# Weights laid out in DRAM by loads, and the first projections taken k tile by k tile

## The chip, the cores and the metric

The kernel runs on one core of a Trainium2 chip. The metric is the time of one execution on the device in microseconds (us). A core has a TensorE for matrix products (PE in the profile; its weight loads are PEld), a VectorE (DVE), a ScalarE (ACT), a GpSimd (POOL), a SyncE (SP) that only issues transfers here, and 16 DMA engines between DRAM and SBUF. Products are summed in eight PSUM banks. Each engine takes its instructions in program order and waits on semaphores of the others.

## The reference

One layer over 256 tokens `x` of width 1024, with 256 context tokens `ctx`. Everything is float32.

```
sh1, sc1, g1, sh2, sc2, g2 = split(silu(c) @ w_mod + b_mod)         # the context: the same with c_ctx
hc = rmsnorm(ctx) * (1 + csc1) + csh1
hx = rmsnorm(x) * (1 + sc1) + sh1
u, q, k, v, g, gates, lr = split(h @ w_in)                          # widths 512 512 512 1024 1024 2048 32
pooled = centred means of u over windows 2, 4, 8, 16, minus u
o = gated linear attention, both directions, of q, k, v, seeded by the context's k and v
x = x + g1 * mixer(pooled, o, g, gates) @ w_o                       # w_pool_br and w_gla_br inside
x = x + g2 * moe(rmsnorm(x) * (1 + sc2) + sh2)                      # 32 experts, 2 of one group per token
return rmsnorm(x) * final_g
```

The weights are 201 MB for the experts (`moe_w1`, `moe_w3`, `moe_w2`), 25 MB for `w_mod` and some 34 MB for the rest. They pass through SBUF once.

## The kernel before

**Stages.** (1) the modulation of the first norm and the projections u, q and half of g of the tokens; (2) k, v, the other half of g, the decays, attention, pooling, gates and the output projection, some 240 us in which the tokens (`hx`) and the context (`hc`) are matmul operands; (3) routing; (4) the experts in 16 pairs, whose hidden products are `hp` (line 1349) and whose outputs are `yp` (line 1382); (5) the last norm.

**Loads.** A load is one transfer of at most 1 MiB into a slot of 128 x 2048 floats (`ld`). The text `LOADS` lists the loads of stages 1 and 2 in order, and the experts' follow. The SP issues them in order; there are 20 slots in lane r (some hold other tiles) and 2 in lane m (for `mod` loads). A load is issued once its slot's last user is done, and eight transfers at most are under way, since each takes one of eight semaphores. `plan_loads` finds the step from which a load may be issued. `f` loads are 256 columns of `w_mod` for all eight k tiles, so each row brings 1 KB runs; `qu` loads are the columns of u and q for two k tiles (4 KB runs); `in` and `g` loads are 512 columns for four k tiles (2 KB runs); `mod` and experts' loads have 8 KB runs.

**Order of work.** The text `WORK` is the program of stages 1 to 3. Each item calls a step function (`steps`), and while it runs, the class `Line` chains each instruction on PE, ACT and DVE behind the last of its engine; so the items' order is the engine's order. A product is made of three passes in a rounded format: `s kind j` casts 1024 weights a partition on ACT (high part), `l kind j` subtracts on DVE (low part), then the products high x high, high x low, low x high run. There are three buffers for such parts (`highs`, `lows`, `third`, two halves each).

**Stage 1.** `s x` squares and sums x (ACT, DVE), `n x` sums over partitions with a matmul against ones (`ss_ps`) and makes the reciprocal root (ACT Ln, Exp; DVE `newton`). `f h j` (`first_cols`) multiplies one load of `w_mod` by the two condition columns, 8 matmuls into a bank `mod`, and copies the 256 columns to `sa`; `t j` (`shifted`) turns them into columns (`mcol`, `amul`) and calls `modulated`: DVE scales x, ACT adds the shift (`hx`, high part), DVE makes the low part; two k tiles at a time. `q j` and `u k` are the products. `i n` puts n idle matmuls of ones on PE (`g<-ones`). For the context there are `s c` (squares), `a c` (three sums), `n c` and `h i`. `e q` and `e u` copy the finished banks out on ACT and give the banks back; `k k 0` and `k k 1` are k's products for tokens and context, and their four banks are those of q and u.

Of the kernel before, what the change touches and what calls it, by code (L numbers as in the profile page):

```python
# [129 lines left out]
def hybrid_block_kernel(  # L130
    ctx: ExitStack,
    tc: tile.TileContext,
    x, xT, cT, vec, w_mod, b_mod, w_in, w_gates, pool_w,
    w_pool_br, w_gla_br, w_o, router_w, router_b,
# [333 lines left out]
    def first_cols(half, j):  # L468

        if half:  # L470
            first_ps[j] = bank("mod0")
        w, ps, hs = need(("first", half, j)), first_ps[j], slice(256 * half, 256 * half + 256)
        sm = sa[:, 512 * (j % 2):512 * (j % 2) + 512]
        with tc.high_priority():
            for k in range(KT):
                g = 32 * (k % 4)
                pe.matmul(ps[g:g + 32, hs], scol[:, k, :], w[:, 256 * k:256 * k + 256],
                               start=(k < 4), stop=(k > 3), tile_position=(0, g))
            if half + j:
                dve.tensor_copy(out=sm[:, hs], in_=ps[:, hs])  # L480
            else:
                act.copy(out=sm[:, hs], in_=ps[:, hs])
        done(("first", half, j))

    def shifted(j):

        ps = first_ps.pop(j)
        k2 = slice(2 * j, 2 * j + 2)
        with tc.high_priority():
            for h in range(2):  # L490
                for i in range(2):
                    n = 256 * h + 128 * i
                    pe.matmul(ps[:, 4 * h + 2 * i:4 * h + 2 * i + 2], sa[:, 512 * (j % 2) + n:512 * (j % 2) + n + 128], sums4,
                                   start=True, stop=True)
            dve.tensor_tensor(out=mcol[:, :, :, k2], in0=ps[:, 0:8].rearrange("p (h i u) -> p h u i", h=2, i=2),
                              in1=bmod[:, :, None, k2].to_broadcast([128, 2, 2, 2]), op=ALU.add)
            dve.scalar_tensor_tensor(out=amul[:, :, k2], in0=mcol[:, 1, :, k2], scalar=1.0,
                                     in1=g1n[:, None, k2].to_broadcast([128, 2, 2]), op0=ALU.add, op1=ALU.mult)
            modulated(xn, banks["rx"], 2 * j, 2, 0, hx)
        if j == 3:  # L500
# [1143 lines left out]
```

## Time and profile before

| | us |
|---|---|
| median of 3 runs (747.81 to 748.62) | 747.84 |
| the profiled execution | 749.17 |
| its span, first to last instruction | 747.5 |
| PE busy | 691.5 (93%) |
| DVE busy | 298.0 (40%) |
| ACT busy | 205.7 (28%) |
| DMA queue of the loads, share of 16 engines | 89.9% |

A busy PE is not PE at its peak, because matmuls are pipelined and their ends are modelled. One float32 matmul stands in the trace as two records; the rounded ones as one. A DMA share a little above 1 means that packets overlap. In the chain that ended last, PE has 69% of the span and transfers of experts' weights 24%; the rest is in single per cents. The page's DMA row, 40 slices of 18.7 us, reads 9, 9, 9, 7, 5, 4, 2, 3, 7 tenths at the start and 9 or 8 from the tenth slice (168 us) to the last but one.

### The profile page before, as it was taken

What the parts mean: (1) busy time and instruction counts of PE and PEld (TensorE: products, weight loads), DVE (VectorE), ACT (ScalarE), POOL (GpSimd) and SP (SyncE); (2) the same over time, 40 slices, a digit from 0 to 9 for tenths busy, and PEclk for the clock granted to TensorE, in tenths of its full rate; (3) what the DMA queues carried; (4) which work ended last, traced back from release to release, by engine and by line L of the source; (5) the groups of instructions that cost most, each with busy time, mean ns of one, the idle gap of its engine ahead of it and who ended that gap; (6) DMA issues with size and microseconds to landing.
All of it is one profiled execution on the core that took longest, in us unless ns stands there. A gap on an engine that the chain in (4) does not pass through costs nothing.

```text
span 747.5 us, 9833 instructions
## 1 busy us (share of the span) xinstructions
PE 691.5 (93%) x3986; PEld 393.9 (53%) x3987; DVE 298.0 (40%) x593; ACT 205.7 (28%) x386; POOL 9.9 (1%) x19
## 2 busy tenths in 40 slices
PE   7999999999999999999989989989989988988884
PEld 6689978879999988433332333322323323222221
DVE  4578986798577686311221021121120120121013
ACT  3354755786554556210010010000000000000012
POOL 0000000010000000000000000000000000000000
PEclk9999999999999999999999999999999999999998
DMA  9997542379998889999999999999999999999993
GB/s 320 362 397 298 182 164 70 120 276 354 344 360 299 331 333 338 347 426 420 422 421 422 420 422 420 422 422 419 420 422 423 420 421 420 421 422 420 422 420 148
DMA packets 55608, 267.42 MB, mean 358 GB/s; under 512 B 4612, under 2 KB 13572, under 8 KB 28804
## 3 DMA queue, kind: packets, MB, share of 16 engines
q1 hardware_dynamic: 54754, 266.45, 89.9%
q8 instruction: 33, 0.54, 0.3%
q10 hardware_dynamic: 804, 0.29, 0.1%
q14 instruction: 17, 0.14, 0.0%
HBM read 265.66 MB, written 1.05 MB: 357 GB/s over the span
## 4 chain that ended last, share of the span: by engine, by line
PE 69%; DMA 25%; DVE 3%; ACT 1%; issue 1%; SPq 0%; ACTq 0%; DVEq 0%
DMA ld<-in_moe_w_dram 24%; PE hp L1349 17%; PE yp L1382 8%; PE v L158 6%; PE xg_ps L1325 3%; PE k L158 3%; PE Y L158 3%; PE wo L158 3%; PE acc L1406 2%; PE g L158 2%; PE u L158 2%; PE q L158 2%; PE V L158 2%; PE U L158 2%; PE X L158 2%; PE T L158 2%
## 5 line engine op out<-in xcount | busy, mean ns | idle before, releaser
L1349 PE MATMUL hp<-ld,bc 128*32 128x512 f32 x1024 | 214.1, 594 | 6.1 <-DMA ld<-in_moe_w_dram 6.1
L1349 PEld LDWEIGHTS hp<-ld,bc 128*32 128x32 f32 x1024 | 57.4, 109 | 144.2 <-issue 126.5
L1382 PE MATMUL yp<-ld,wk 128*32 128x512 f32 x512 | 113.9, 632 | 2.9 <-DMA ld<-in_moe_w_dram 2.9
L1361 ACT COPY wk<-hp 128x256 f32<-128x256 f32 x16 | 5.9, 368 | 210.0 <-PE hp L1349 210.0
L158 DVE TENSOR_TENSOR lows<-ld,highs 128x1024 fp32r<-128x1024 f32 x46 | 56.1, 1221 | 14.7 <-ACT highs L158 14.6
L1382 PEld LDWEIGHTS yp<-ld,wk 128*32 128x32 f32 x512 | 25.8, 113 | 64.8 <-issue 54.8
L1389 DVE TENSOR_TENSOR yb<-yp,bc 64x512 f32<-64x512 f32 x32 | 22.0, 689 | 94.4 <-PE yp L1382 94.0
L1331 ACT ACTIVATE bc<-xg_ps,mcol 128x128 f32<-128x128 f32 x32 | 14.2, 456 | 159.2 <-PE hp L1349 148.2
L158 ACT CAST highs<-ld 128x1024 fp32r<-128x1024 f32 x46 | 48.2, 1052 | 32.5 <-DMA ld<-in_w_in_dram 8.8
L1362 DVE COPY wk<-hp 128x256 f32<-128x256 f32 x16 | 6.8, 424 | 125.9 <-ACT wk L1361 125.9
L1325 PE MATMUL xg_ps<-wr,h 128*128 128x128 f32 x256 | 35.9, 286 | 9.5 <-DVE wk L1370 5.3
L1325 PEld LDWEIGHTS xg_ps<-wr,h 128*128 128x128 f32 x256 | 30.6, 191 | 25.0 <-issue 7.5
L1336 DVE TENSOR_SCALAR bc<-xg_ps,mcol 128x128 f32<-128x128 f32 x32 | 12.3, 408 | 77.0 <-PE hp L1349 73.2
L158 DVE SCALAR_TENSOR_TENSOR macc<-ld,sj,macc 128x1024 f32<-128x1024 f32 x32 | 40.3, 1279 | 0.4 <-DMA ld<-in_w_mod_dram 0.4
L1406 PE MATMUL acc<-yb,wk 128*128 128x512 f32 x64 | 29.5, 604 | 5.5 <-DVE yb L1389 5.5
L158 ACT ACTIVATE gx<-gx 128x256 f32<-128x256 f32 (+2 forms) x56 | 24.8, 484 | 4.7 <-DVE gx L158 3.7
L1406 PEld LDWEIGHTS acc<-yb,wk 128*128 128x128 f32 x64 | 11.5, 189 | 23.4 <-DVE yb L1389 15.2
L1366 PE MATMUL hT<-cst,wk 128*128 128x128 f32 x64 | 13.6, 299 | 10.3 <-ACT wk L1361 10.0
L1313 DVE TENSOR_TENSOR yb<-cst,rank 128x128 f32<-128x128 f32 (+1 forms) x32 | 7.4, 254 | 38.1 <-PE woT L1397 27.1
L1366 PEld LDWEIGHTS hT<-cst,wk 128*128 128x128 f32 x64 | 6.5, 140 | 28.0 <-ACT wk L1361 22.7
L158 PE MATMUL wo<-highs,ot 128*128 128x512 f32 (+1 forms) x80 | 20.0, 354 | 0.0
L158 PE MATMUL Y<-ot,highs 128*128 128x256 f32 x128 | 18.3, 285 | 0.0
(318 smaller groups left out, 913.2 us busy)
## 6 DMA issues: line engine op xcount, KB each, us to landing
ld<-in_moe_w_dram SPq DMA_DIRECT2D x191, 1024.0 KB, 19.8
ld<-in_w_mod_dram SPq DMA_DIRECT2D x24, 1024.0 KB, 5.3
ld<-in_w_in_dram SPq DMA_DIRECT2D x22, 1024.0 KB, 8.7
ld<-in_w_o_dram SPq DMA_DIRECT2D x4, 1024.0 KB, 8.9
ld<-in_w_gla_br_dram SPq DMA_DIRECT2D x4, 1024.0 KB, 9.2
ld<-in_w_pool_br_dram SPq DMA_DIRECT2D x2, 1024.0 KB
ld<-in_xT_dram SPq DMA_DIRECT2D x1, 1024.0 KB
ld<-in_cT_dram SPq DMA_DIRECT2D x1, 1024.0 KB
```

Of the source, the lines that this page charges most:

```text
L158: i = f(*args, **kwargs)
L1313: dve.tensor_tensor(out=wo[:, t, i:i + m], in0=slots_of[:, None, :].to_broadcast([128, m, CAP]), in1=rank[:, t, n:n + m, None].to_broadcas ...
L1325: i = pe.matmul(pv[:, kk, :], h2[:, t, 2 * kp + kk, :], oh[:, t].rearrange("p e s -> p (e s)"), start=(t == 0), stop=(t == 1))
L1331: act.activation(out=xg[:, kp, kk], in_=pv[:, kk], func=AF.Identity, scale=am2[:, 1, 2 * kp + kk:2 * kp + kk + 1], bias=sh2[:, 1, 2 * kp + ...
L1336: mark["xg"] = dve.tensor_scalar(out=xg[:, kp, kk], in0=pv[:, kk], scalar1=am2[:, 1, k:k + 1], scalar2=sh2[:, 1, k:k + 1], op0=ALU.mult, o ...
L1349: mark["hp"] = pe.matmul(hp[o:o + CAP, :], xs(e, k), w[:, 512 * (k % 4):512 * (k % 4) + 512], start=(k == 0), stop=(k == KT - 1), tile_pos ...
L1361: act.copy(out=hs[:, 0:2], in_=hv[:, 0:2])
L1362: dve.tensor_copy(out=hs[:, 2:4], in_=hv[:, 2:4])
L1366: pe.transpose(out=tp[:, 128 * k:128 * k + 128], in_=hs[:, k, :], identity=ident)
L1382: pe.matmul(yp[r:r + CAP, :], hid[:, 2 * k + e, :], w[:, o:o + 512], start=(k == 0), stop=(k == 3), tile_position=(0, r))
L1389: dve.tensor_tensor(out=wk["yb"][rs, os], in0=yp[rs, :], in1=g2bc[rs, os], op=ALU.mult)
L1406: pe.matmul(acc[t, n], wT[:, 256 * n + 128 * t:256 * n + 128 * t + 128], wk["yb"][:, 512 * n:512 * n + 512], start=False, stop=last)
```

## The change

Three things change together.

- **Layout.** The host lays out `w_first` (8 blocks of 128 x 2048: the 128 shift and the 128 scale columns of one k tile, for all eight input tiles) and `w_blocks` (34 blocks, one for each load of `w_in`, `w_pool_br`, `w_gla_br`, `w_o`), so that each of these loads is one run of 6 or 8 KB in a row. `w_mod` loses its first 2048 columns. The bytes are the same. x comes in two halves.
- **Blocks of u, q and g.** `qu 0` to `qu 3` now hold one k tile each: u and q (1024) and 512 columns of g. `qu 4` and `qu 5` hold u and q of two k tiles. The load `g 0` is gone. `s a k` and `l a k` split u and q of one k tile, `s b k` and `l b k` split g's 512.
- **Order.** `f k`, `t k`, `q k`, `u k`, `g k` now run k tile by k tile, `t k` for one tile. `mod` loads come behind the first `in` loads. The items from `h 1` on stand as they stood.

```diff
-LOADS = """vec, x, f 1 0, f 0 0, cst, qu 0, f 1 1, qu 1, f 0 1, ...
+LOADS = """vec, x, f 0, cst, qu 0, f 1, qu 1, f 2, qu 2, f 3, qu 3, f 4, f 5, qu 4, f 6, f 7, qu 5, ctx, in 1024 0, gates,
...
-WORK = """s x, i 16, f 1 0, i 3, n x, i 2, f 0 0, s q 0, t 0, l q 0, ...
+WORK = """s x 0, i 16, s x 1, n x, f 0, s a 0, l a 0, t 0, s b 0, l b 0, q 0, f 1, s a 1, u 0, t 1, l a 1, g 0, s b 1, l b 1,
...
+    t 7, u 6, l a 7, s c, s k 0, mz 0 0, a c, l k 0, q 7, u 7, mz 0 1, n c, e q, s k 1, l k 1, e u, mods, k 0 0, h 0, k 1 0,
...
+    def block(*key):
+        return w_blocks[BLOCKS.index(key)]
...
         elif kind == "f":
-            c0 = n[0] * D + 256 * n[1]
-            plan(("first", *n), wm[:, :, c0:c0 + 256], 8)
+            plan(("first", *n), w_first[n[0]], 1)
...
         elif kind == "qu":
-            plan(("qu", *n), wi[:, 2 * n[0]:2 * n[0] + 2, 0:D], 2)
+            plan(("qu", *n), block("qu", *n), 1)
+            if n[0] < 4:
+                size["qu", *n] = 1536
         elif kind in ("g", "in"):
             c0, hf = ([2560] + n)[-2:]
-            plan((c0, hf), wi[:, hf * 4:hf * 4 + 4, c0:c0 + 512], 4)
+            plan((c0, hf), block(c0, hf), 1)
...
-    pieces.update({("e", NE - 1, 2, 1): 2})
+    pieces.update({("e", NE - 1, 2, 1): 2, "xT": 2})
...
+    def first_cols(k):
+
+        w, ps = need(("first", k)), bank("mod0")
+        first_ps[k] = ps
+        for i in range(KT):
+            g = 32 * (i % 4)
+            pe.matmul(ps[g:g + 32, 0:256], scol[:, i, :], w[:, 256 * i:256 * i + 256],
+                      start=(i < 4), stop=(i > 3), tile_position=(0, g))
+        dve.tensor_copy(out=sa[:, 256 * (k % 2) + 512:256 * (k % 2) + 768], in_=ps[:, 0:256])
+        done(("first", k))
+
+    def shifted(k):
+
+        ps, o = first_ps.pop(k), 256 * (k % 2) + 512
+        for h in range(2):
+            pe.matmul(ps[:, 256 + 2 * h:258 + 2 * h], sa[:, o + 128 * h:o + 128 * h + 128], sums4, start=True, stop=True)
+        dve.tensor_tensor(out=mcol[:, :, :, k], in0=ps[:, 256:260].rearrange("p (h u) -> p h u", h=2),
+                          in1=bmod[:, :, k:k + 1].to_broadcast([128, 2, 2]), op=ALU.add)
+        dve.tensor_scalar(out=amul[:, :, k], in0=mcol[:, 1, :, k], scalar1=1.0, scalar2=g1n[:, k:k + 1], op0=ALU.add, op1=ALU.mult)
+        modulated(xn, banks["rx"], k, 1, 0, hx)
...
     def step_s(kind, j=None):
         if kind == "x":
-            squares(xn, qu)
+            a, b = (slice(1024 * j + 512 * i, 1024 * j + 512 * i + 512) for i in range(2))
+            act.activation(out=qu[:, a], in_=xn[:, a], func=AF.Square)
+            dve.tensor_tensor(out=qu[:, b], in0=xn[:, b], in1=xn[:, b], op=ALU.mult)
+            dve.tensor_tensor(out=qu[:, a], in0=qu[:, a], in1=qu[:, b], op=ALU.add)
+            if j == 0:
+                banks["ss"] = bank("ss_ps")
+            for i in range(2):
+                o = 1024 * j + 256 * i
+                pe.matmul(banks["ss"][:, 0:T], ones, qu[:, o:o + T], start=(j + i == 0), stop=(j + i == 2))
...
-    def step_q(j):
+    def step_q(k):
         accs_of("q"), accs_of("u")
-        for i in range(2):
-            feat(accs_of("q"), [halves["q", j][0][i]], [hx[p][:, 2 * j + i, :] for p in range(2)], 2 * j + i == 0, 2 * j + i == KT - 1, 2)
+        feat(accs_of("q"), [w_of("q", k)], [hx[p][:, k, :] for p in range(2)], k == 0, k == KT - 1, 2)
```

The order of PE's first matmuls, up to the first product of q (`ss_ps` is the sum of squares of x, `g<-ones` the idle matmuls, `mod` the modulation). Before:

```order
L158 MATMUL g<-ones 128x128 x16
L158 MATMUL mod_153<-ld,sj 32x256 x8
L158 MATMUL g<-ones 128x128 x3
L158 MATMUL ss_ps<-qu,ones 128x256
L158 MATMUL g<-ones 128x128 x2
L158 MATMUL mod_153<-ld,sj 32x256 x8
L158 MATMUL mod_153<-cst,sa 128x2 x4
L158 MATMUL g<-ones 128x128 x10
L158 MATMUL mod_211<-ld,sj 32x256 x8
L158 MATMUL q<-hx_70,highs 128x256 x4
```

And PE's first matmuls of the changed kernel, which is the same place:

```order
L163 MATMUL ss_ps<-qu,ones 128x256 x2
L163 MATMUL g<-ones 128x128 x16
L163 MATMUL ss_ps<-qu,ones 128x256 x2
L163 MATMUL mod_166<-ld,sj 32x256 x8
L163 MATMUL mod_166<-cst,sa 128x2 x2
L163 MATMUL q<-hx_70,third 128x256 x4
```

The sixteen idle matmuls move from the head of PE's queue to between the two halves of the sum of squares, the other fifteen are gone, and one load of `w_mod` instead of three stands ahead of the first product.

PE again, from the last products of u to the first of k, where `ss_ps<-kT` is the sum of squares of the context. Before:

```order
L158 MATMUL u<-third,hx_70 128x512 x2
L158 MATMUL g<-highs,hx_70 128x512 x2
L158 MATMUL g<-highs,hx_71 128x512 x2
L158 MATMUL g<-lows,hx_70 128x512 x2
L158 MATMUL g<-highs,hx_70 128x512 x2
L158 MATMUL g<-highs,hx_71 128x512 x2
L158 MATMUL g<-lows,hx_70 128x512 x2
L158 MATMUL ss_ps<-kT,ones 128x256
```

Behind it come two more steps of g, then k. The same place of PE's queue in the changed kernel, from the last small matmuls of the modulation:

```order
L163 MATMUL mod_461<-cst,sa 128x2 x2
L163 MATMUL u<-highs,hx_70 128x512 x2
L163 MATMUL u<-highs,hx_71 128x512 x2
L163 MATMUL u<-lows,hx_70 128x512 x2
L163 MATMUL q<-hx_70,highs 128x256 x4
L163 MATMUL q<-hx_71,highs 128x256 x4
L163 MATMUL q<-hx_70,lows 128x256 x4
L163 MATMUL u<-highs,hx_70 128x512 x2
L163 MATMUL u<-highs,hx_71 128x512 x2
L163 MATMUL u<-lows,hx_70 128x512 x2
L163 MATMUL ss_ps<-kT,ones 128x256
L163 MATMUL k<-hx_70,third 128x256 x4
```

The four steps of g that stood on both sides of the context's sum have moved to the front; behind `t 7` only u, q, u are left ahead of that sum, and k follows it at once.

ACT at the same place, from the squares of the context to its modulation (`qu<-q` and `qu<-u` are `e q` and `e u`, `kT<-ss_ps` and `kT<-kT` the Ln and Exp of the context's norm). Before:

```order
L158 ACTIVATE qu<-q 128x256 x4
L158 ACTIVATE kT<-ld 128x1024
L158 CAST highs<-ld 128x1024
L158 COPY qu<-u 128x512 x2
L158 CAST third<-ld 128x1024
L158 ACTIVATE kT<-ss_ps,epst 128x256
L158 ACTIVATE kT<-kT 128x256
L158 CAST highs<-ld 128x1024
L158 ACTIVATE hc_72<-ld,mcol 128x256 x8
```

ACT in the changed kernel, from the squares of the context as well:

```order
L163 ACTIVATE kT<-ld 128x1024
L163 CAST third<-ld 128x1024
L1053 DMA macc<-in_b_mod_dram 1x2048
L163 ACTIVATE kT<-ss_ps,epst 128x256
L163 ACTIVATE kT<-kT 128x256
L163 ACTIVATE qu<-q 128x256 x4
L163 CAST highs<-ld 128x1024
L163 COPY qu<-u 128x512 x2
L163 ACTIVATE hc_72<-ld,mcol 128x256 x8
```

Both copies out of the banks, `qu<-q` and `qu<-u`, moved from ahead of the context's Ln and Exp to behind them.

## Rows read from the trace of the kernel before

**Rows 1.** The chain of waits: start us, us, what.

```profile
544.16 20.49 DMA ld<-in_moe_w_dram
```

**Rows 2.** By stretch: us, busy PE, PEld, DVE, ACT, POOL; clock, DMA share, GB/s.

```profile
71.50:155.70 84.20, 84.20 (x471) 70.83 (x470) 65.49 (x98) 54.74 (x111) 4.30 (x9) 1.00 0.38 130
155.70:308.00 152.30, 150.33 (x1106) 136.33 (x1105) 113.48 (x213) 88.70 (x151) 2.46 (x3) 1.00 0.92 339
308.00:308.80 0.80, 0.80 (x9) 0.80 (x9) 0.00 (x0) 0.00 (x0) 0.00 (x0) 1.00 0.00 0
308.80:734.70 425.90, 385.62 (x1906) 128.62 (x1904) 66.19 (x178) 27.38 (x64) 0.00 (x0) 0.98 1.01 418
```

**Rows 3.** Issues of experts' loads, 233 to 308 us, then 320 to 730 us.

```profile
ld<-in_moe_w_dram SPq DMA_DIRECT2D x24, 1024.0 KB, 6.5
...
ld<-in_moe_w_dram SPq DMA_DIRECT2D x161, 1024.0 KB, 19.8
```

**Rows 4.** What SP's queue waited for longest, 72 to 155 us.

```profile
SPq L311 <- DVE macc L158: 49.7, 7, 17.5
```

**Rows 5.** Instructions in order of time, start of the program.

```profile
1.09 6.02 PE L158 MATMUL g<-ones 128*128 128x128 f32 x32 [1.09 <-DVE ones L375]
...
6.40 1.22 DVE L158 TENSOR_TENSOR qu<-ld 128x1024 f32<-128x1024 f32 x1 [2.87 <-DMA ld<-in_xT_dram]
...
9.54 1.93 PE L158 MATMUL mod<-ld,sj 128*32 128x256 f32 x16 [2.42 <-DMA ld<-in_w_mod_dram]
...
13.33 0.47 ACT L158 ACTIVATE qu<-ss_ps,epst 128x256 f32<-128x256 f32 x1 [5.87 <-PE ss_ps L158]
...
15.20 0.42 DVE L158 SCALAR_TENSOR_TENSOR qu<-qu 128x256 f32<-128x256 f32 x1
...
16.14 2.48 PE L158 MATMUL g<-ones 128*128 128x128 f32 x20
...
19.55 1.21 PE L158 MATMUL q<-hx,highs 128*128 128x256 f32 x8
```

**Rows 6.** By stretch, columns as in rows 2.

```profile
9.10:12.50 3.40, 2.96 (x21) 1.78 (x22) 1.44 (x3) 0.00 (x0) 0.00 (x0) 0.50 1.11 367
```

**Rows 7.** Groups by form, 0 to 80 us: busy us, mean ns, idle before.

```profile
L158 DVE TENSOR_TENSOR lows<-ld,highs 128x1024 fp32r<-128x1024 f32 x10 | 12.1, 1218 | 0.0
L158 ACT CAST highs<-ld 128x1024 fp32r<-128x1024 f32 x10 | 10.4, 1047 | 8.4 <-DMA ld<-in_w_in_dram 7.7 <-PE k L158 0.6
...
L158 ACT ACTIVATE qu<-q 128x256 f32<-128x256 f32 x4 | 1.2, 391 | 1.9 <-PE q L158 1.9
L158 ACT COPY qu<-u 128x512 f32<-128x512 f32 x2 | 1.1, 622 | 0.0
...
L158 DVE TENSOR_TENSOR qu<-qu 128x512 f32<-128x512 f32 x1 | 0.7, 692 | 0.0
```

**Rows 8.** The chain of waits, 28 to 72 us.

```profile
28.07 0.18 DVE mcol L158
...
28.99 0.52 ACT hx L158
...
39.09 1.00 PE mod L158 x16
...
44.28 0.79 PE mod L158 x8
45.06 5.86 PE q L158 x48
50.92 2.75 PE u L158 x12
...
59.56 11.51 PE k L158 x96
```

**Rows 9.** Instructions in order of time, from the context's sums.

```profile
52.90 2.41 DVE L158 TENSOR_TENSOR kT<-kT 128x1024 f32<-128x1024 f32 x3 [0.91 <-ACT kT L158]
...
62.27 1.60 PE L158 MATMUL k<-hc,third 128*128 128x256 f32 x12
```

More of the change, by code (lines that the diff above doesn't have):

```diff
@@ L65 @@
 V_N = 80
+BLOCKS = ([("qu", i) for i in range(6)] + [(c, h) for c in range(1024, 5632, 512) for h in range(2)]
+          + [("wp", i) for i in range(2)] + [("wg", i) for i in range(4)] + [("wo", n, h) for n in range(2) for h in range(2)])
 class _Dry:
@@ L245, in hid_tile @@
         return wk["in"][:, o:o + 256]
-    parts = {"n": 0, "of": 3}
+    parts = {"n": 4, "of": 3}
     def part():
@@ L308, in issue @@
         if len(src.shape) == 2:
-            m = 2048 // pieces.get(key, 1)
-            for o in range(0, 2048, m):
+            n = size.get(key, 2048)
+            m = n // pieces.get(key, 1)
+            for o in range(0, n, m):
                 nc.sync.dma_start(out=t[:, o:o + m], in_=src[:, o:o + m])
@@ L433, in summed, with rstd_rows @@
             dve.tensor_tensor(out=w[:, 0:m], in0=w[:, 0:m], in1=w[:, m:2 * m], op=ALU.add)
-    def rstd_rows(w):
-        ps = bank("ss_ps")
-        pe.matmul(ps[:, 0:T], ones, w[:, 0:T], start=True, stop=True)
+    def rstd_rows(w, ps=None):
+        if ps is None:
+            ps = bank("ss_ps")
+            pe.matmul(ps[:, 0:T], ones, w[:, 0:T], start=True, stop=True)
         r, m, q = (w[:, 256 * i:256 * i + 256] for i in (4, 5, 6))
@@ L466, in hybrid_block_kernel @@
     first_ps = {}
[L468 to L490, printed above, removed]
-                for i in range(2):
[L492 to L500, printed above, removed]
+    def first_cols(k):
[7 more added lines that the diff above has]
+        done(("first", k))
@@ new lines, in shifted @@
+    def shifted(k):
[6 more added lines that the diff above has]
+        modulated(xn, banks["rx"], k, 1, 0, hx)
+        if k == KT - 1:
@@ L623, in half_of @@
         t = need(key)
-        return t.rearrange("p (k n) -> p k n", k=2)[:, :, 512 * i:512 * i + 512] if key[0] == "qu" else t[:, 1024 * i:1024 * i + 1024]
+        if key[0] == "qu" and j < 4:
+            return t[:, 0:1024] if kind == "a" else t[:, 1024:1536]
+        return t[:, 1024 * i:1024 * i + 1024]
     @step
@@ L651, in step_n @@
     def step_n(kind):
-        banks["r" + kind] = rstd_rows(qu if kind == "x" else kw)
+        banks["r" + kind] = rstd_rows(qu, banks["ss"]) if kind == "x" else rstd_rows(kw)
     @step
@@ L675, in w_of @@
     def w_of(kind, k):
+        if kind in ("q", "u"):
+            return halves["a", k][0][kind == "q"]
+        if kind == "g" and k < 4:
+            return halves["b", k][0][0]
         return halves[kind, k // 2][0][k % 2]
@@ L1594, in _laid_out, with blocked @@
     vec[:, 72:80] = np.asarray(inputs["norm2_g"]).reshape(128, KT)
-    w_in = squeezed("w_in")
+    w_in, w_mod = squeezed("w_in"), squeezed("w_mod")
+    def blocked(w, ks, cs):
+        return np.concatenate([np.concatenate([w[128 * k:128 * k + 128, c:c + n] for c, n in cs], axis=1) for k in ks], axis=1)
+    blocks = np.zeros((len(BLOCKS), 128, 2048), x.dtype)
+    for b, key in zip(blocks, BLOCKS):
+        if key[0] == "qu":
+            i = key[1]
+            v = blocked(w_in, [i], [(0, D), (2560, 512)]) if i < 4 else blocked(w_in, [2 * i - 4, 2 * i - 3], [(0, D)])
+        elif key[0] in ("wp", "wg"):
+            v = blocked(squeezed({"wp": "w_pool_br", "wg": "w_gla_br"}[key[0]]), [2 * key[1], 2 * key[1] + 1], [(0, D)])
+        else:
+            w, c, hf = (squeezed("w_o"), 512 * key[1], key[2]) if key[0] == "wo" else (w_in, *key)
+            v = blocked(w, range(4 * hf, 4 * hf + 4), [(c, 512)])
+        b[:, 0:v.shape[1]] = v
+    first = np.stack([blocked(w_mod, range(KT), [(128 * k, 128), (D + 128 * k, 128)]) for k in range(KT)])
     gates = np.zeros((128, 1280), x.dtype)
@@ L1603, in _laid_out @@
     return {
[L1604 to L1606 removed]
+        "x": x, "xT": turned(x), "cT": turned(squeezed("ctx")), "vec": vec, "w_first": first,
+        "w_mod": w_mod[:, 2 * D:], "b_mod": np.asarray(inputs["b_mod"]).reshape(1, -1), "w_blocks": blocks, "w_gates": gates,
+        "pool_w": squeezed("pool_w"),
         "router_w": np.ascontiguousarray(router.reshape(KT, 128, 36).transpose(1, 0, 2)).reshape(128, KT * 36),
```

34 lines of the change are left out of this document (11 added, 23 removed).

## Prediction

> **What bounds the kernel now.** I read the chain of waits from its end first, then the table by stretch, then the issues of loads, then the instructions of the first 72 us.
>
> The chain shows what holds the end. From 544 us on its pieces are transfers of the experts' weights, nine of about 20 us up to 731 us with little between; one stands in [rows 1]. The table by stretch says the same: from 308.8 to 734.7 us the DMA share is 1.01 at 418 GB/s [rows 2], the DMA engines hardly rest, and an expert's load lands 19.8 us after its issue because eight are queued [rows 3]. So the end is the moment at which this stream is through, and some 13 us behind it.
>
> When does the stream start to be late? At 308.0 to 308.8 us the share is 0.00 [rows 2]: the queue had run dry, every free slot had been filled. Up to there the SP waits for slots. In 233 to 308 us a load lands 6.5 us after its issue, against 19.8 later [rows 3]; in 71.5 to 155.7 us the share is only 0.38 while PE is busy for the whole 84.2 us [rows 2], and the SP's queue waits for DVE's uses of `mod` loads [rows 4], which lie in the order of work. So up to 308 us the loads follow the compute, and that is PE: 150.3 of 152.3 us busy even in the second stretch [rows 2].
>
> Hence one rule for the sum: a shift of the compute at the place where the old and new order meet again (k on the context) goes through to the end in full, since no transfer debt lies between there and 308 us. In the kernel before, that first product of k on `hc` begins at 62.27 us [rows 9]. The question is when it begins now.
>
> **The layout.** The bytes are the same, the runs longer. By itself it makes a load land sooner, and a load that lands sooner is worth something only where PE waits for it. In stage 1 PE has 41 us of work from the first q on (below) while all loads up to `qu 5`, 14.2 MiB, need 14.2 x 2.51 = 36 us at 418 GB/s; so from the first q on PE is the slower of the two, and later the SP waits for slots. I cost the layout at 0 beyond the start; the rival below takes the other view.
>
> **The start, up to the first q.** Before, it begins at 19.55 us [rows 5]. Now:
>
> - x was whole at 6.40 [rows 5]; half a MiB at 418 GB/s is 1.25 us, so the first half is there at 5.15.
> - DVE squares 512 and adds 512, 0.69 each [rows 7]: 6.55. Two sums on PE begin at 6.6.
> - The sixteen idle matmuls ran from 1.09 us, before x came, and cost nothing. Now they stand behind the first two sums and ahead of the last two. They are 32 records; 20 such records took 2.48 us later, 0.124 each [rows 5], so 4.0 us. A sum has twice the columns, 0.5 us. But the 32 took 6.02 us at the start [rows 5], 2.05 us more than at 0.124: a start from rest. PE now rests until 6.6, so I add the 2.05: 6.6 + 1.0 + 4.0 + 2.05 = 13.65, and the last two sums end at 14.65.
> - From Ln to the finished root it took 15.62 - 13.33 = 2.3 us [rows 5]: 16.95.
> - DVE is in order: the copy of `f 0` (0.42, as its other ops of 256), the low part of a 0 (1.22, rows 7), then columns, scaling and shift, 29.51 - 28.07 = 1.44 [rows 8]. First q at 20.05, 0.5 later than before, though two loads of `w_mod` and a second small step no longer stand ahead of it.
>
> Bounds: without the 2.05 it is 18.0; with all of 6.0 us (sums and idle matmuls) at half speed, 24.0. I take 20.05, since the row of the start is a start from rest too.
>
> On this term the trace shows: when PE had idled from 7.1 to 9.5 us, the granted clock read 0.50, which is 1.2 GHz, from 9.1 to 12.5, and the sixteen records of `mod` took 1.93 us where later ones take 1.00 [rows 5, 6, 8]. The clock column does not show the slow start from 1.09 us; the records do. The Trainium skill, "TensorE: Matmul & The Clock Gate", Part 1, puts it as "the default state is throttled, and activity releases the throttle": by that rule the idle matmuls behind a wait are paid for at the low clock first, and it speaks against the new place. By it the first q is at 20 us; by a clock that is full at once it would be at 18.0 and the end 2.05 us earlier than forecast.
>
> **From the first q to k on the context.** Work on PE by [rows 8]: a step of q 5.86/4 = 1.465, of u 2.75/2 = 1.375, of g the same shape, of `f` 1.00, of the small columns 0.79 for two tiles, so 0.40 for one, of k 11.51/8 = 1.44, the context's sum 0.5.
>
> Now: 8 q 11.7, 8 u 11.0, 4 g 5.5, 7 f 7.0, 7 t 2.8, sum 0.5, 2 k 2.9: 41.4 us. Before: the same with 5 f and 3 double t, 39.0, in 62.27 - 19.55 = 42.7, so 3.7 of it waits. If nothing waited now, k on the context would begin at 61.5, 0.8 earlier.
>
> But look at what is behind `t 7`. Count from the end of its matmuls. DVE: hx's high part is there at 1.44, its low part at 1.95; low part of a 7 (1.22) 3.15; the context's squares (1.22) 4.4; the three sums, 2.41 [rows 9], 6.8. PE meanwhile has only u 6 (to 1.4), q 7 (its last pass needs the low part, to 3.65) and u 7 (to 5.0): it idles 1.8 us and runs the context's sum at 6.85 to 7.35. Now ACT, in its new order: Ln and Exp, 0.47 and about 0.42, to 8.3; four copies of q, 1.2, to 9.5; a cast, 1.05, to 10.6; two copies of u, 1.1 [rows 7], to 11.7. The first four matmuls of k write four banks, the ones of q and u, so the fourth waits for 11.7. Eight of twelve remain, 0.96, to 12.7, one more step of k, 14.1: k on the context. Its operand is ready at 12.9 (DVE: low part of k 1 behind the cast, two scalings, ACT's shift), so that does not bind. Without waits the same work is 7.7 us. The waits cost 6.4.
>
> Before, the four steps of g on both sides of that sum covered all this: the copies of q and u were done by the time k began. Their cover, 4 x 1.375 = 5.5 us, has been spent earlier, where PE had other work.
>
> The idle stretches, 1.8 and then parts of 4.4 us, may drop the clock as the 2.4 us at 7.1 did; a stretch of 3.4 us at 1.2 GHz costs up to 1.7 [rows 6]. I take half of one, 0.85, between 0 and 1.7.
>
> **The sum.** 20.05 + 41.4 + 6.4 + 0.85 = 68.7, against 62.27: 6.4 us later. The profiled execution took 749.17 with its span of 747.5; its median sibling is 747.84, 1.33 less. 749.17 + 6.4 - 1.33 = 754.2 us. From the bounds: -2.05 and -0.85 give 751.3, +3.95 and +0.85 give 759.0.
>
> **Rivals.**
>
> 1. The waits behind `t 7` are covered: ACT and DVE run ahead and the banks are free in time. Then 20.05 + 41.4 = 61.5, -0.8, so 747.0: no change that counts. For it: DVE and ACT are busy for only 40% and 28% of the span. Against it: both are in order, and everything named above hangs on the last columns of `t 7`. Chance 0.06.
> 2. The transfers absorb it: the stream is the bound from 155.7 us on, and a later compute is only waited for less. Then 747.8. For it: share 0.92 in 155.7 to 308 us; against it: 0.00 at 308.0 [rows 2]. Chance 0.05.
> 3. The layout pays, faster. Place: 155.7 to 308 us. There 339 GB/s x 152.3 us = 51.6 MB pass; at 418 they take 123.5 us, 28.8 less. If transfers, not slots, held the stream there, it could be up to 28.8 us ahead at 308; half of that gives 754.2 - 14.4 = 739.8. It decides once it gives more than 6.4 us. For it: 6.5 us from issue to landing is more than one load's own time. Against it: a queue that has run dry at 308 us keeps no debt, and the SP waits there for DVE and PE. Chance 0.08.
>
> That the change doesn't do as it says I leave aside: its order is fixed by the chaining of the engines.
>
> **The numbers.** My forecast, with its own bounds: 0.81. Time 754.2. The range: 750.5 to 759.0, from the bounds with a little below for a shorter wait; it leaves out the rivals, 0.19 in sum. What a measurement of this kernel can tell from no change is about 0.2%, 1.5 us: faster than 746.3 has 0.08 (rival 3), within it 0.11 (rivals 1 and 2), slower 0.81.
>
> **What would show it.** The first q near 20 us, with the idle matmuls between 7 and 14 us; PE without waits for DMA between 20 and 55 us; behind the last u a wait of 1.5 to 2 us for DVE's sums and then one of 3 to 5 us in the first step of k for ACT; the first k on `hc` near 69 us; a DMA share of 0 shortly before 316 us and 418 GB/s behind it; the last load some 6 us later than 734.7. A first q by 18 us or copies of q ahead of the context's Ln would make my sum wrong, a stream that never runs dry before the experts would make its rule wrong, and a share near 1.01 with a queue at 300 us would be rival 3.

## The result, and the profile after

The changed kernel takes 759.57 us (median of 4 runs, 758.61 to 760.6), the kernel before beside it 748.23 (747.81 to 750.11): a ratio of 1.0145, with a 95% interval of 1.013 to 1.016. It is 11.3 us slower. The forecast was 6.4 us slower, 754.2, with a range of 750.5 to 759.0: the direction was right, the size little more than half, the time just outside the range. The profiled execution took 760.6 (749.17 before), its span is 758.9.

Whether the stream of weights follows the compute is read first. By stretch, the changed kernel at the places of [rows 2], some 11.4 us later, and one stretch more; columns as there:

```profile
82.40:167.20 84.80, 84.80 (x476) 71.41 (x475) 65.11 (x97) 55.36 (x111) 4.34 (x9) 1.00 0.37 128
167.20:315.20 148.00, 146.03 (x1085) 134.86 (x1084) 110.02 (x184) 87.54 (x145) 2.44 (x3) 1.00 0.90 340
319.46:320.26 0.80, 0.80 (x9) 0.80 (x9) 0.00 (x0) 0.00 (x0) 0.00 (x0) 1.00 0.27 113
320.30:746.20 425.90, 385.63 (x1905) 128.25 (x1904) 66.29 (x178) 27.41 (x64) 0.00 (x0) 0.98 1.01 418
...
274.20:274.80 0.60, 0.60 (x7) 0.60 (x6) 0.56 (x2) 0.38 (x1) 0.00 (x0) 1.00 0.00 0
```

The two long stretches have the shares and rates of before, 0.37 for 0.38 and 0.90 for 0.92, and the last one is as long as before to the digit, 425.9 us at 418 GB/s. Everything from 82 us on is the old kernel, later. The share of 0.00 that I looked for shortly before 316 did not come. With the shift that was measured, the place of 308.0 to 308.8 us is 319.46 to 320.26, and there the share is 0.27: the queue has nearly run dry, not quite. The 0.00 at 274.2 is another place; the kernel before has it too, 11.5 us earlier (262.70 to 263.30). The issues show the rule more plainly. The SP's queue in the kernel before, and then in the changed one:

```profile
307.86 0.80 SPq L311 DMA_DIRECT2D ld<-in_moe_w_dram  x2
```

```profile
319.32 0.84 SPq L317 DMA_DIRECT2D ld<-in_moe_w_dram  x2
```

The same two loads are issued 11.46 us later, as a slot comes free from the compute. The median time from issue to landing there is 7.0 us (6.5 before, rows 3) and 19.8 later, as before:

```profile
ld<-in_moe_w_dram SPq DMA_DIRECT2D x23, 1024.0 KB, 7.0
...
ld<-in_moe_w_dram SPq DMA_DIRECT2D x167, 1024.0 KB, 19.8
```

So the loss arises in the first 82 us. The start in order of time, to be held against [rows 5]:

```profile
4.63 0.69 DVE L163 TENSOR_TENSOR qu<-ld 128x512 f32<-128x512 f32 x1 [1.18 <-DMA ld<-in_xT_dram]
...
6.18 2.08 PE L163 MATMUL ss_ps<-qu,ones 128*128 128x256 f32 x4 [6.18 <-DVE qu L163]
...
8.04 5.43 PE L163 MATMUL g<-ones 128*128 128x128 f32 x32
...
17.06 0.61 PE L163 MATMUL mod<-cst,sa 128*128 128x2 f32 x4 [1.72 <-DVE sa L163]
...
19.60 2.93 PE L163 MATMUL q<-hx,third 128*128 128x256 f32 x12 [1.93 <-ACT hx L163]
...
22.46 1.94 PE L163 MATMUL mod<-ld,sj 128*32 128x256 f32 x16
```

The idle matmuls stand between the halves of the sum and take 5.43 us. The first q begins at 19.60, forecast 20.05. Then its twelve matmuls take 2.93 us where later ones take 1.70, and the sixteen of `mod` 1.94 for 1.07. The stretches of low clock, columns as in [rows 2]:

```profile
18.40:25.20 6.80, 5.60 (x30) 4.02 (x31) 2.17 (x5) 1.96 (x3) 0.53 (x1) 0.50 1.02 429
...
66.20:73.00 6.80, 5.00 (x19) 4.25 (x20) 5.66 (x12) 5.14 (x12) 0.00 (x0) 0.50 0.99 376
```

Two of them in the first 100 us, 6.8 us each at 0.50, which is 1.2 GHz; before there were two of 3.4 us, one of them in [rows 6]. The chain of waits, one k tile without g, against [rows 8]:

```profile
46.03 1.00 PE mod L163 x16
47.03 1.63 PE q L163 x12
48.67 0.34 PE mod L163 x4
49.01 1.49 PE u L163 x6
50.50 1.00 PE mod L163 x16
```

4.47 us from one `mod` to the next. And the change to k, in order of time, against [rows 9]:

```profile
57.44 0.51 PE L163 MATMUL mod<-cst,sa 128*128 128x2 f32 x4
...
62.37 2.41 DVE L163 TENSOR_TENSOR kT<-kT 128x1024 f32<-128x1024 f32 x3
...
62.69 0.62 PE L163 MATMUL u<-lows,hx 128*128 128x512 f32 x2
...
64.92 0.67 PE L163 MATMUL ss_ps<-kT,ones 128*128 128x256 f32 x2 [1.62 <-DVE kT L163]
...
66.46 1.19 ACT L163 ACTIVATE qu<-q 128x256 f32<-128x256 f32 x4
...
67.15 1.13 PE L163 MATMUL k<-hx,third 128*128 128x256 f32 x2 [1.56 <-ACT qu L163]
...
68.45 1.10 ACT L163 COPY qu<-u 128x512 f32<-128x512 f32 x2
...
69.12 4.77 PE L163 MATMUL k<-hx,third 128*128 128x256 f32 x22 [0.84 <-ACT qu L163]
...
73.73 1.60 PE L163 MATMUL k<-hc,third 128*128 128x256 f32 x12
```

PE waits 1.62 us for DVE's sums, 1.56 for ACT's copies of q, 0.84 for those of u, and then does 22 matmuls of k in 4.77 us. k on `hc` begins at 73.73, 11.46 later than the 62.27 of [rows 9].

### The profile page after: what moved, and what is told of

Read it like the earlier page. It is cut to its first block, busy times and chain, and to the rows that moved or that the text cites. A ratio compares the mean times of both kernels' runs of the same rounds, so it can differ in the third digit from the quotient of the medians.

```text
span 758.9 us, 9801 instructions
## 1 busy us (share of the span) xinstructions
PE 693.6 (91%) x3962; PEld 392.8 (52%) x3963; DVE 300.3 (40%) x604; ACT 206.1 (27%) x388; POOL 9.9 (1%) x19
## 4 chain that ended last, share of the span: by engine, by line
PE 73%; DMA 19%; DVE 5%; ACT 2%; issue 1%; SPq 0%; DVEq 0%; ACTq 0%
PE hp L1356 19%; DMA ld<-in_moe_w_dram 18%; PE yp L1389 9%; PE v L163 6%; PE xg_ps L1332 4%; PE k L163 3%; PE Y L163 3%; PE wo L163 3%; PE acc L1413 3%; PE g L163 2%; PE V L163 2%; PE U L163 2%; PE X L163 2%; PE T L163 2%; PE W L163 2%; PE q L163 1%
## 5 line engine op out<-in xcount | busy, mean ns | idle before, releaser
L163 DVE TENSOR_TENSOR lows<-ld,highs 128x1024 fp32r<-128x1024 f32 (+1 forms) x47 | 55.6, 1187 | 15.2 <-ACT highs L163 15.1
L163 ACT CAST highs<-ld 128x1024 fp32r<-128x1024 f32 (+1 forms) x47 | 47.9, 1024 | 27.4 <-PE wo L163 6.7
L1413 PEld LDWEIGHTS acc<-yb,wk 128*128 128x128 f32 x64 | 11.5, 189 | 23.4 <-DVE yb L1396 15.2
## 6 DMA issues: line engine op xcount, KB each, us to landing
ld<-in_moe_w_dram SPq DMA_DIRECT2D x191, 1024.0 KB, 19.8
```

The source lines that it names most:

```text
L163: i = f(*args, **kwargs)
L1413: pe.matmul(acc[t, n], wT[:, 256 * n + 128 * t:256 * n + 128 * t + 128], wk["yb"][:, 512 * n:512 * n + 512], start=False, stop=last)
```

## The experiments

All were timed beside the kernel before. The table has the anchors of each trace (us): the first q, the first k on `hc`, `lr` (the first product of the decays, behind the eight steps of k), and the span; then the median and the ratio to before with its interval. The anchors are of one profiled execution each, which lies up to 1.4 us from its kernel's median.

| kernel | first q | k on hc | lr | span | median | ratio |
|---|---|---|---|---|---|---|
| before | 19.55 | 62.27 | 70.91 | 747.5 | 748.1 to 748.6 | 1 |
| changed | 19.60 | 73.73 | 82.37 | 758.9 | 759.57 | 1.0145 (1.013, 1.016) |
| b1_delay | 19.29 | 66.50 | 75.14 | 751.7 | 752.36 | 1.0057 (1.0041, 1.0074) |
| a3_old_layout_stage2 | 19.54 | 73.64 | 82.27 | 759.0 | 760.44 | 1.0159 (1.0142, 1.0176) |
| b2_layout_alone | 17.68 | 60.39 | 69.03 | 745.5 | 746.81 | 0.998 (0.9966, 0.9994) |
| a1_idle_head | 15.81 | 69.68 | 78.84 | 755.6 | 757.42 | 1.0125 (1.0109, 1.0142) |
| a2_banks_first | 19.25 | 69.54 | 78.31 | 755.0 | 756.94 | 1.0123 (1.0106, 1.0139) |
| a4_fill_start | 19.57 | 71.79 | 80.83 | 757.5 | 758.4 | 1.013 (1.0113, 1.0147) |
| a5_fill_both | 19.73 | 69.87 | 78.51 | 754.8 | 756.68 | 1.0114 (1.0096, 1.0132) |
| d1_cover_back | 19.04 | 68.37 | 77.05 | 753.3 | 755.69 | 1.0103 (1.0083, 1.0122) |
| c1_two_repairs | 14.08 | 64.04 | 72.81 | 750.1 | 751.87 | 1.0049 (1.0032, 1.0066) |
| c2_three_more | 14.11 | 67.94 | 76.71 | 753.3 | 756.09 | 1.0107 (1.0088, 1.0126) |
| c3_chained_load | 14.13 | 62.98 | 71.75 | 747.9 | 751.05 | 1.0031 (1.0019, 1.0043) |
| b3_layout_fill | 17.65 | 58.99 | 67.64 | 744.0 | 746.13 | 0.9966 (0.9952, 0.9979) |

From `lr` to the end of the span it is 676.2 to 677.3 us in all fourteen traces, while `lr` itself moves by 14.7. That is the rule of the prediction in one column.

**Does a delay at k pass to the end?** (b1_delay)

```diff
-... mods, s k 1, g 2, g 3, k 0 0,        (the kernel before)
+... mods, s k 1, g 2, g 3, I 20, k 0 0,  (I n: n idle matmuls of ones in a bank of their own)
```

> The kernel before, with twenty idle matmuls (20 x 0.248 = 5.0 us) in a bank of their own just ahead of the first step of k; nothing else. This tests the rule of the sum. Theory A (a shift of the compute in front of k goes through to the end in full): 748.2 + 5.0 = 753.2 us. Rival (the stream of transfers absorbs it): 748.2.

Its trace, PE in order of time:

```profile
59.16 4.63 PE L158 MATMUL idle<-ones 128*128 128x128 f32 x40
...
66.50 1.60 PE L158 MATMUL k<-hc,third 128*128 128x256 f32 x12
```

k on `hc` is 4.23 us later, the span 4.2, the median 4.2. The delay came out shorter than the 5.0 us meant, but it arrives in full. The rule holds, and rival 2 (transfers absorb it) falls.

**Is it the layout?** (a3_old_layout_stage2, b2_layout_alone) The first is the changed kernel with the loads of stage 2 in the old strided form, the second the kernel before with all loads in blocks:

```diff
-            plan((c0, hf), block(c0, hf), 1)                                         (a3)
+            plan((c0, hf), w_in.rearrange("(k p) n -> p k n", p=128)[:, hf * 4:hf * 4 + 4, c0:c0 + 512], 4)
-            plan(("first", *n), wm[:, :, c0:c0 + 256], 8)                            (b2)
+            plan(("first", *n), w_first[4 * n[0] + n[1]], 1)
```

> The changed kernel, but the loads of in, g, wp, wg and wo blocks come from the weights as they were, in runs of 2 and 4 KB; the loads of stage 1 (first, qu) stay as in the change. Theory A (slots, not transfers, hold the loads up to 308 us): 759.6 within 0.2%. Theory B (the layout matters in the middle): a changed time, faster by some us if the new layout hurts, slower by up to 28.8 us if it helps.

> The kernel before with the new layout alone: each load of w_in, w_pool_br, w_gla_br, w_o and of the first 2048 columns of w_mod is one contiguous block, the order of work and of loads is the old one. Theory A (the change's loss is its order; the layout is worth nothing beyond the start): k on hc between 61.3 and 62.3, time 747 to 748.5. Rival B (long runs make the loads land sooner where PE waits for them, and this pays through the whole kernel): below 745. Rival C (the layout itself costs, and the order less than I think): above 750.

With the strided loads back, k on `hc` and the time are those of the changed kernel. With blocks alone the kernel before gets 0.2% faster (interval 0.06 to 0.34%). Where, its start shows:

```profile
8.76 1.07 PE L160 MATMUL mod<-ld,sj 128*32 128x256 f32 x16 [0.92 <-DVE qu L160]
...
17.68 1.22 PE L160 MATMUL q<-hx,highs 128*128 128x256 f32 x8
```

In [rows 5] `mod` waited 2.42 us for its load and ran at the low clock; now it waits 0.92, for DVE. The first q is 1.87 earlier, k on `hc` 1.88: all the layout gives is given at the start. Little of it is the clock: in the trace of b1_delay, which has the old loads and starts like the kernel before, the clock reads 1.00 from 9.1 to 12.5 us, and the first q still begins 1.61 later than here (19.29). So the order, with the blocks cut for it, costs 12.8 us (759.57 - 746.81), and rival 3 falls.

**The two places of the order.** (a1_idle_head, a2_banks_first)

```diff
-"""s x 0, i 16, s x 1, n x,                                (a1)
+"""i 16, s x 0, s x 1, n x,
-q 7, u 7, mz 0 1, n c, e q, s k 1, l k 1, e u, mods,      (a2)
+q 7, u 7, mz 0 1, e q, e u, n c, s k 1, l k 1, mods,
```

> The changed kernel with the sixteen idle matmuls back at the head of PE's queue, ahead of both halves of the sum of squares; nothing else. Theory A (order of work: late start, two stretches at the low clock, waits behind t 7): the sums are done near 9 us instead of 14.3, the root near 11.5, the first q at about 15 instead of 19.60; the low clock may come earlier or stay. k on the context begins 4 to 5 us earlier than 73.73, the time is about 755 us. Theory B (the layout or the transfers cost the time, PE only follows): the first q moves, the end does not: 759.6.

> The changed kernel with the copies of q and u out of their banks put ahead of the context's Ln and Exp on ACT; nothing else. Theory A: k's first step can begin right behind the context's sum, near 65.7 us, its first four matmuls do not wait for ACT; k on the context begins near 69.5 instead of 73.73 (then the context's own chain, Ln, Exp, newton, scaling, holds it), so the time is 4 us less, about 755.5 us; if the low clock from 66.2 us stays, 756.5. Theory B: 759.6.

With the idle matmuls at the head the first q is 3.8 earlier, k on `hc` 4.05. With the copies first, PE in order of time:

```profile
64.40 0.67 PE L163 MATMUL ss_ps<-kT,ones 128*128 128x256 f32 x2 [1.61 <-DVE kT L163]
64.72 3.21 PE L163 MATMUL k<-hx,third 128*128 128x256 f32 x24
...
69.54 1.74 PE L163 MATMUL k<-hc,third 128*128 128x256 f32 x12 [1.60 <-ACT hc L163]
```

The wait for DVE's sums stays (1.61), the waits for the copies are gone, and a new one for `hc` (1.60) takes part of their place. There is also no low clock here: 24 matmuls in 3.21 us. The gain at k on `hc` is 4.2. Both times are above those that I had expected, and neither kernel tells what the clock has by itself.

**The clock by itself.** (a4_fill_start, a5_fill_both) Idle matmuls fill PE's waits, and the order of all else stays: first ahead of the first q, then at the change to k too.

```diff
-n x, f 0, s a 0, l a 0, t 0, s b 0, l b 0, q 0,                   (a4 and a5)
+n x, f 0, s a 0, l a 0, I 7, t 0, I 8, s b 0, l b 0, q 0,
-q 7, u 7, mz 0 1, n c, e q, s k 1,                                (a5)
+q 7, u 7, I 6, mz 0 1, n c, I 14, e q, s k 1,
```

> The changed kernel with idle matmuls of ones in PE's two waits ahead of the first q: seven steps between the first load of the modulation and its small columns, eight between these and q. Theory A (what my sum missed at the start is the clock: 6.8 us at 0.50 from 18.4 us on, because PE waits 1.72 and 1.93 us just ahead): the first q stays at 19.6 to 19.9, the stretch at 0.50 behind it goes, the last u ends near 60.6 instead of 63.3, k on hc begins 2.5 to 2.7 earlier, and the time is 757 us. Rival B (the slow first steps wait for operands or weights, or the clock falls whatever PE does there): a stretch at 0.50 of the same length stays in the first 30 us, and the time is that of the changed kernel, 759 to 760.

> The kernel of a4_fill_start (idle matmuls in the waits ahead of the first q) with idle matmuls in PE's waits at the change to k as well: six steps behind the last u, fourteen behind the context's sum. The order of all other work is that of the changed kernel. Theory A (the second stretch at 0.50, 65.9 to 72.7 us, follows from PE's waits and costs 2.4 us): no stretch at 0.50 before 100 us, the waits for the copies of q and u are still there, the first product of the decays (lr) begins at 78.4 to 79 instead of 80.8, time 756 us. Rival B (the second stretch costs nothing, since those steps wait for ACT and DVE anyway): lr at 80.5 or later, time 758 to 759.

a4_fill_start, PE from the second filler, then its clock by stretch (columns as in [rows 2]):

```profile
17.50 2.03 PE L163 MATMUL idle<-ones 128*128 128x128 f32 x16
19.57 1.74 PE L163 MATMUL q<-hx,third 128*128 128x256 f32 x12
...
60.20 0.61 PE L163 MATMUL u<-lows,hx 128*128 128x512 f32 x2
...
66.65 5.34 PE L163 MATMUL k<-hx,third 128*128 128x256 f32 x22 [1.04 <-ACT qu L163]
```

```profile
18.40:25.20 6.80, 6.77 (x54) 5.41 (x53) 3.00 (x8) 1.97 (x3) 0.53 (x1) 1.00 1.02 424
```

The first q begins where it did and takes 1.74 instead of 2.93; the granted clock from 18.4 to 25.2 us is 1.00, and the last products of u begin 2.49 us earlier (60.20 for 62.69). k on `hc` gains 1.94 of it: the second stretch at 0.50 is still there, 65.9 to 72.7 us, and now all 22 matmuls of k lie in it (5.34 us for 4.77). a5_fill_both, PE at the change to k:

```profile
63.08 3.29 PE L163 MATMUL idle<-ones 128*128 128x128 f32 x28
66.12 0.48 PE L163 MATMUL k<-hx,third 128*128 128x256 f32 x2
66.77 3.27 PE L163 MATMUL k<-hx,third 128*128 128x256 f32 x22 [0.17 <-ACT qu L163]
69.87 1.60 PE L163 MATMUL k<-hc,third 128*128 128x256 f32 x12
```

The third matmul of k still waits for ACT, until 66.77 (66.65 in a4_fill_start); but 22 matmuls take 3.27 us for 5.34, and `lr` comes 2.32 earlier. In a5_fill_both the granted clock of the first 100 us is 1.00. Theory A holds for the first q, the stretches, the last u and `lr`; k on `hc` in a4_fill_start (1.94 earlier, 2.5 to 2.7 expected) and both times (758.4 and 756.68, expected 757 and 756) fall short of it. Together the two stretches cost 3.86 us at k on `hc` (73.73 to 69.87) and at `lr` (82.37 to 78.51), and 4.1 of the span. The medians fall by less, 1.2 and 2.9 us, and the intervals of the ratios still meet that of the changed kernel, so the size is read from the traces. That the stretches are not of these traces alone shows in the mean granted clock of each execution: 0.975 to 0.978 in the four of the changed kernel, 0.983 in all four of a4_fill_start, 0.985 to 0.989 in a5_fill_both.

**The cover.** (d1_cover_back) On top of a4_fill_start, two of g's four early steps stand on both sides of the context's sum again; the queue of ACT keeps the copies behind the context's Ln and Exp.

```diff
-g 1, s b 2, l b 2, f 3, ng, q 2, ... u 2, l a 3, g 2, s b 3, l b 3, ... u 3, l a 4, g 3, f 5,
+g 1, f 3, q 2, ... u 2, l a 3, ... u 3, l a 4, f 5,
-l k 3, z 0 0,
+l k 3, ng, z 0 0,
-t 7, u 6, l a 7, s c, s k 0, mz 0 0, a c, l k 0, q 7, u 7, mz 0 1, n c, e q,
+t 7, u 6, l a 7, s c, s b 2, l b 2, mz 0 0, s b 3, a c, l b 3, q 7, u 7, g 2, s k 0, l k 0, mz 0 1, n c, g 3, e q,
```

> The kernel of a4_fill_start with two of g's four early steps (k tiles 2 and 3, with their casts) moved back to both sides of the context's sum, as cover for PE there; the copies of q and u still stand behind the context's Ln and Exp. In a4_fill_start k on hc began at 71.8, lr at 80.8, time 758.4. Theory A (the change spent PE's cover for the chain behind t 7; that chain hangs on DVE and ACT and starts 2.9 us earlier once two steps of g are out of its way, while PE has 2.9 us of work beside it): k on hc at 67.5 to 69, no wait at the context's sum or under 1 us, time 754 to 755.5. Rival B (PE's total work sets the place, the waits only move): k on hc at 71 or later, time 757.5 or more.

```profile
59.61 0.67 PE L163 MATMUL ss_ps<-kT,ones 128*128 128x256 f32 x2 [0.68 <-DVE kT L163]
...
68.37 1.64 PE L163 MATMUL k<-hc,third 128*128 128x256 f32 x12
```

These are rows of PE. The wait at the sum is 0.68, k on `hc` 3.42 earlier than in a4_fill_start, the same products done. Of the 3.42, 0.58 lie in the 22 matmuls of k (4.76 us for 5.34): a stretch of 3.4 us at 0.51 (65.1 to 68.5) remains, half as long as in a4_fill_start. The time is 0.2 above what theory A gave.

**Do the losses add, and can this order win?** (c1_two_repairs, c2_three_more, c3_chained_load)

```diff
-"""s x 0, i 16, s x 1, n x, f 0, s a 0, l a 0, t 0, s b 0,      (c1; with the edit of a2)
+"""i 16, s x 0, s x 1, n x, f 0, s a 0, t 0, l a 0, s b 0,
-f 0, s a 0, t 0, l a 0, ... l a 5, f 6, ... l a 6, f 7, ...     (c2, on top of c1)
+f 0, s a 0, I 5, t 0, I 4, l a 0, ... l a 5, s c, f 6, ... l a 6, a c, f 7, ... l a 7, n c,
-            act.dma_start(out=mstate["next"][-1][0:1, :], ...)  (c3, on top of c2)
+            load = nc.scalar.dma_start(out=mstate["next"][-1][0:1, :], ...)
+            after(load, act.last)
+            act.last = load
```

In c2 the load of the context also moves ahead of `f 7`, and `ng`, which hands four slots to another lane, behind `l k 3`, as in d1_cover_back.

> The changed kernel with the idle matmuls at the head of PE's queue again, the copies of q and u ahead of the context's norm, and the columns of k tile 0 ahead of DVE's low part. Each of the first two alone brought k on hc from 73.7 to 69.6. Theory A (they are two separate losses, one at the start, one at the change to k, and they add): k on hc at 64 to 65.5, with 1 to 2 less from the third edit 63 to 65; time 749 to 751. Rival B (both take away the same loss, the second stretch at half clock, or DVE's sums take the place of the waits): k on hc at 67 or later, time 753 or more.

> The previous one (two repairs) with idle matmuls in PE's waits ahead of the first q, the context loaded earlier, and its squares, sums and norm done during the steps of k tiles 5 to 7, so that PE goes from u to k without waiting for DVE's sums. Theory A (the stretch at 0.50 and the waits for the sums are the rest of the loss): no stretch at 0.50 before k, no wait at ss_ps of the context, k on hc at 60 to 61.5, time 745.5 to 747, which is below the kernel before. Rival B (DVE and ACT, in order, are then late for the columns of k tiles 6 and 7, and what is saved at the sums is lost there): k on hc not below 63, time 749 or more.

> The kernel of c2_three_more with one edit: the small load of b_mod that ACT issues is chained into ACT's order at its place, behind the cast of k 0, instead of standing ahead of the cast of k tile 6, where ACT waited 7.88 us for POOL's zeroing of its target. Theory A (that one instruction at the head of ACT's queue was the whole failure of that kernel): PE's waits of 4.07 and 1.38 us in q of k tiles 6 and 7 go, the last u ends at 56 to 57, k on hc begins at 59.5 to 61, time 745.5 to 747.5. Rival B (the context's squares and sums on ACT and DVE hold the columns of k tiles 5 to 7 back anyway): k on hc at 63 or later, 749.5 or more.

c1_two_repairs: k on `hc` at 64.04, so the two losses add; the time is 0.9 above the range expected. The numbers of c2_three_more are those of rival B, but the cause is a third one. POOL, ACT and PE in order of time:

```profile
49.60 1.80 POOL L1057 MEMSET macc<- 128x2048 f32 x1 [49.12 <-PE mod L163]
51.44 0.53 ACTq L1060 DMA_DIRECT2D macc<-in_b_mod_dram  x1
52.06 1.04 ACT L163 CAST highs<-ld 128x1024 fp32r<-128x1024 f32 x1 [7.88 <-POOL macc L1057]
...
53.57 2.08 PE L163 MATMUL q<-hx,highs 128*128 128x256 f32 x8 [4.07 <-ACT hx L163]
```

The chaining that keeps WORK's order leaves DMA issues out. Freed by the new order, a small load that ACT issues had moved ahead of the cast of k tile 6; it waited for POOL's zeroing, which waited for a slot that `f 7` still read, and ACT behind it for 7.88 us, PE 4.07. Chained to its place (c3_chained_load), k on `hc` begins at 62.98, between the two theories and near B:

```profile
50.14 2.40 DVE L163 TENSOR_TENSOR kT<-kT 128x1024 f32<-128x1024 f32 x3
52.46 0.41 DVE L163 COPY sa<-mod 128x256 f32<-128x256 f32 x1
52.93 0.61 PE L163 MATMUL mod<-cst,sa 128*128 128x2 f32 x4 [1.77 <-DVE sa L163]
```

DVE and PE again: the context's sums stand ahead of the columns of k tile 7, and PE waits 1.77 us for them there instead of 1.6 behind the last u. With these repairs this order is at 751.05, 0.2 to 0.4% above the kernel before. The profile is of the fastest of six runs. The cover of d1_cover_back is not among the repairs; whether the order wins with it too was not run, and what is left against b2_layout_alone (2.59 us at k on `hc`) was not taken apart.

**A version below both.** (b3_layout_fill) The old order, the new layout, and idle matmuls in the two waits of about 0.55 us ahead of the one early stretch at 0.50 that is left.

```diff
-f 0 1, l u 1, t 1, f 1 2, l q 1, s u 2, u 2,
+f 0 1, I 3, l u 1, t 1, f 1 2, l q 1, s u 2, I 3, u 2,
```

> The kernel before with the new layout, and idle matmuls (three steps each) in PE's two waits of about 0.55 us ahead of the stretch at 0.50 from 27.7 to 31.1 us. Theory A: that stretch goes, k on hc begins 1 to 1.5 us earlier than with the layout alone (60.4), at 59 to 59.4, time 745.5. Rival B (PE's waits there are longer than the idle matmuls, or the stretch moves to another place): k on hc at 60 or later, time 746.5 to 747.

PE behind the second filler:

```profile
27.12 0.94 PE L160 MATMUL idle<-ones 128*128 128x128 f32 x6
27.81 1.18 PE L160 MATMUL u<-highs,hx 128*128 128x512 f32 x4
```

The same four matmuls of u in b2_layout_alone:

```profile
27.68 2.07 PE L160 MATMUL u<-highs,hx 128*128 128x512 f32 x4 [0.52 <-ACT hx L160]
```

The stretch is gone, k on `hc` is 1.40 earlier, and the kernel takes 746.13 us, between the two theories and 0.34% (0.21 to 0.48) less than before. The step from b2_layout_alone is seen in one trace of each; the intervals of the two times overlap, and the mean granted clock over all runs is 0.984 in both, so a gain in time from this filler is not shown.

## Why the prediction was wrong in size

- **The rule** (a shift of k on `hc` goes to the end in full): right. The shift is 11.46, the span is 11.4 longer, and b1_delay shows it for a delay made on purpose. The sign named for it, a share of 0 shortly before 316, did not come; at the place that moved with the compute it is 0.27.
- **The layout at 0 beyond the start**: right (a3_old_layout_stage2), and the start's part, 1.87 us in the old order, had no term of its own.
- **The first q**: 20.05 forecast, 19.60 measured, in part by luck: the first two sums took 2.08 us where 1.0 stood, the idle matmuls 5.43 where 6.05 stood, and x was there half a microsecond earlier.
- **The step that failed: "I take half of one, 0.85, between 0 and 1.7"**, the clock. I gave it to the change to k alone and sized it by the 3.4 us of [rows 6]. The runs show two stretches of 6.8 us. One is at a place that I had not looked at: my own sum has PE wait for columns, scaling and shift just ahead of the first q, and I priced that wait, but not what it does to the products behind it. It cost 2.49 us at the last u (a4_fill_start). The other cost 1.51 at k on `hc`: from the end of `t 7` it is 15.78 us to there in the changed kernel and 14.27 in a5_fill_both. Filled together they gave back 3.86 us at k on `hc`, where 0.85 stood.
- **The steps in between**, a second and smaller error. From the first q to the end of `t 7` I had 20.05 + 41.4 - 7.7 = 53.75, so 33.7 us; it took 38.35 (19.60 to 57.95), 4.65 more, of which 2.49 is the clock. The rest, 2.16, is the steps: 4.47 us a k tile without g, where 1.00 + 1.465 + 0.40 + 1.375 is 4.24, about 0.2 in each of eight, and 0.33 more in the second k tile (in a4_fill_start it takes 6.16 us, later ones with g 5.83). I had taken q and u from runs of several steps on end; alternating, each costs more (1.63 for 1.465, 1.49 for 1.375).
- **The waits behind `t 7`**: right nearly to the row. Counted from 57.95, the sums end at 6.83 (forecast 6.8), the copies of q at 9.7 (9.5), those of u at 11.6 (11.7). Only the matmuls of k behind them were at half clock: 15.78 to k on `hc`, with 14.1 + 0.85 forecast, and 14.27 in a5_fill_both at the full clock. d1_cover_back shows that g's steps were cover: two of the four, put back, gave 3.42 us.

The account at k on `hc`: 68.7 - 0.45 (first q) + 4.65 + 0.83 (15.78 - 14.95) = 73.73. Of the 5.0 us missed, 3.15 are the clock (2.49 + 1.51 - 0.85), 2.16 the steps, 0.17 the waits behind `t 7` (14.27 - 14.1), less the 0.45.

The page of the Trainium skill that I weighed, "TensorE: Matmul & The Clock Gate", says in Part 1 that "the default state is throttled, and activity releases the throttle". The 6.8 us at 0.50 behind PE's waits of 1.72 and 1.93 us, gone once these were filled, point the same way. I had used the rule for the moved idle matmuls alone, and it bears on PE's other waits in the chain too.

## What to carry to other kernels

Where a new order makes PE wait, price the wait twice: the time itself, and, as a bound, the products behind it at half clock; and look for it ahead of each first product, not only at the place that worries you. Work that has no deadline (here g) was worth most beside the longest chain of small operations on in-order engines, so before such work is moved, count what it covers. An order written out by hand holds only for what it chains: one small load that stood too early in an engine's queue cost 5.0 us (756.09 against 751.05).

## What the hardware showed that I had not expected

- The clock fell behind short waits: 1.72 and 1.93 us ahead of 6.8 us at 0.50 in the changed kernel, two of about 0.55 us ahead of 3.4 us in b2_layout_alone. Filled with idle matmuls, neither stretch came. In c1_two_repairs waits of 1.16 and 1.58 us stood ahead of only 3.4 us.
- The length of a wait does not settle it. In a2_banks_first waits of 1.61 and 1.60 us, with 24 matmuls of k between them, left the clock at 1.00. In the trace of b1_delay, which starts like the kernel before, the first `mod` waited 2.66 us for its load and the clock stayed at 1.00 from 9.1 to 12.5 us, where it read 0.50 in [rows 6] behind 2.42 us. So one trace does not show that a stretch comes in every execution, and what sets whether it comes and how long it lasts is open.
- A full clock column is no proof of speed: from the start of the changed kernel to 18.4 us it reads 1.00, and yet 32 records of idle matmuls took 5.43 us there, 0.17 each, where [rows 5] has 0.124 for later ones.
